# Rotary key rows by transfers on SyncE's queue, and four buffers for the squares of q blocks, in the opening of an attention stage

## The chip, the core and the metric

The kernel runs on one core of one Trainium2 chip. A core has TensorE (matmuls; PE in the profile, PEld its weight loads), VectorE (DVE), ScalarE (ACT), GpSimd (POOL) and SyncE (SP), which here only issues transfers. Each engine works through a list of instructions of its own in order; semaphores tie the lists together. Work tiles live in SBUF (128 partitions), results of matmuls in PSUM. The metric is the device time of one execution in microseconds (us), lower is better.

## The reference

One inference step of a two-layer decoder for a prompt of 1024 tokens (with 16 learned tokens ahead) and for 8 samples of 4 new tokens each. Layer A is a convolution module and a feed-forward network with a short convolution. Then one latent (128 wide) and one rotary key (32 wide) are formed for every token. Layer B attends to them and ends with a second feed-forward network. The part at hand, cut to what matters:

```python
q = einsum('btl,lhd->bthd', rms_norm(xn @ w_dq, ...), w_uq)      # 16 heads of 64 + 32
q_nope, q_rope = rms_norm(q[..., :64]), rope(rms_norm(q[..., 64:]))
k_nope = rms_norm(einsum('btc,chd->bthd', c, w_uk))              # from the latent c
v      = einsum('btc,chd->bthd', c, w_uv)
s = (q_nope . k_nope + q_rope . kr) * SM_SCALE                   # kr: one rotary key for all heads
o = softmax(causal(s)) @ v                                       # prompt
# samples: the same attention, over 2048 past tokens in 16 pages per sample and the 4 new ones
```

All in float32.

## The kernel before, in words

`run` calls, one after the other, the convolution phase, the first feed-forward network, `latents`, `attention` (the prompt), `samples`, `project` and the second feed-forward network. Precise products are made of three fast ones: `split` writes a tile as a high part (ACT, L135) and a low part (DVE, L136), and `mm3` multiplies high by high, low by high and high by low (L151).

**Order.** The text of the program is not the order on an engine. A planner with a timeline of its own sets each engine's list from priorities and from what has to be free: a tile can be written only when the last reader of whatever lay at its address before is done. `samples` opens under a high priority (`SPRIO`), so the planner lets its first instructions run among the last heads of `attention` wherever their tiles are free.

**Opening of attention.** `latents` leaves the rotary key rows of all 1040 tokens as a high and a low tile, kth0 and ktl0 (rows 0 to 31), and brings a copy to rows 32 to 63 of a second pair, kth1 and ktl1 (L1094). Attention keeps two sets of key tiles, so that one pair of heads can be prepared while another is in use; the second set (k2h, k2l, named `tiles`) needs the same rotary rows, copied at L1429 and L1431. In before GpSimd does all six copies. Heads go in groups of four. For a group, `group_k` makes keys (raw keys L1157, squares L1159, sums of squares L1160, norm L255 to L260, scaling L1169), `group_q` makes q in nine blocks of tokens: a block's matmuls (L151), two evictions by ACT (L1193, L1194), its squares by ACT (L1196), and their sums by DVE (L1200, L1201); then the norm and the rotation (`rope`, L1103 to L1107) on DVE. `query(n)` transposes the q of head n (L1277, L1280), `scores(n)` finds the largest score of each row (matmul L1307, maximum on DVE L1309 to L1314), `shift(n)` puts it into a row of q (L1323), and `values(n, g)` makes the weights (L1347 to L1350, exponential on ACT L1354) and the products with v (L1337). Opening means: all of group 0, then the nine blocks of group 1 woven into `query(0)` and `scores(0)`. From there the heads follow each other.

**Closing.** After heads 2p and 2p+1 their output is evicted into a tile `o` (L1364). Pairs 0 to 6 go through `finish` (division by way of GpSimd, then L1385 writes `o` to memory); pair 7, the last, through `close(7, 0)` and `close(7, 1)`: reciprocal (L1369) and product (L1370) on DVE, then a transfer on ACT's queue (L1371).

**Samples.** `samples` loads the key weights in two halves into tiles `rx` (L1516, on GpSimd's queue), splits them, turns the samples' q with them (24 small matmuls, `sn<-rx,wh` and the like), and goes through four pairs of samples: `scores(sp)` on pages that SyncE loads (`pg`, L613; splits `ch`, `cl`, and `kh`), `values(sp)` (L1629, L1640, L1651).

**Memory.** A pool is a stretch of SBUF with so many buffers of each tile's name, and pools are laid one behind the other in the order in which they are opened. In `attention` that is, at its end: `bp` (2 buffers; `scr` is there, a 1024-wide work tile that the squares of k and q and the rotation share), `bx` (`PB` = 4 buffers; weights `pf`), `ax` (`trit`, `pick`), `ao` (2 buffers of `o`). The pools of `samples` follow in the same memory.

Of the kernel before, what the change touches and what calls it, by code (L numbers as in the profile page):

```python
# [9 lines left out]
F32 = mybir.dt.float32  # L10
# [108 lines left out]
class Prog:  # L119
# [828 lines left out]
    def latents(self, es, eq, xh, xl, sq):  # L948
        nc, a, o = self.nc, self.a, self.o
# [8 lines left out]
        r = lambda w, n: aq.tile([128, w], F32R, name=n)  # L958
# [9 lines left out]
        with ExitStack() as e2:  # L968
# [113 lines left out]
            h, l = [t[64:96] for t in self.kt[0]]  # L1082
# [8 lines left out]
                for at, w, src in parts:  # L1091
                    self.split(h[:, at:at + w], l[:, at:at + w], ps[:32, src:src + w])
            for t, x in zip(self.kt[1], (h, l)):
                nc.gpsimd.tensor_copy(t[32:64], x.bitcast(F32))  # L1094

    def rope(self, tmp, kind, m, bs, n, d1, d2, x):
        nc = self.nc
# [11 lines left out]
    def attention(self, es):  # L1109
        nc, a = self.nc, self.a  # L1110
# [3 lines left out]
        bp = self.pool(es, "bp", 2)  # L1114
        bx = self.pool(es, "bx", PB)
# [7 lines left out]
        f32 = lambda shape, n, pool=at, **k: pool.tile(shape, F32, name=n, **k)  # L1123
# [9 lines left out]
        def sub(t, m, b0, nb, lo, step, w):  # L1133
            v = t[:m, b0:b0 + nb]
            return bass.AP(v.tensor, v.offset + lo, [list(v.ap[0]), [224, 2 * nb], [step, 2], [1, w]])

        def part(name, src, w, pool=ag):
            raw = f32([128, w], name + "r", pool)
            nc.sync.dma_start(raw, src)
            h, l = f32r([128, w], name + "h", pool), f32r([128, w], name + "l", pool)  # L1140
            self.split(h, l, raw)
            return h, l
# [36 lines left out]
        def group_q(g):  # L1179
            q = st["qn"] = f32([128, NB, 2, 224], f"q{g % 2}", au if g % 2 else ag)  # L1180
            ss, rr = f32([128, 2, 36], "ssq", al), f32([128, 2, 36], "rrq", al)
            nc.gpsimd.memset(ss, 1.0)
            nc.gpsimd.memset(q[:, :, :, 96:128], 0.0)
            wq = [part(f"wq{k}", a["wuq"][k][:, 384 * g:384 * g + 384], 384) for k in range(2)]
            yield
            for b in range(NB):
                m = 128 if b < 8 else 64
                c0 = 128 * b
                ps = (ps_p if g or b > EARLY else ps_f).tile([128, 512], F32, name="p")[:m, :384]
                for k in range(2):  # L1190
                    self.mm3(ps, self.qlh[k][:, c0:c0 + m], self.qll[k][:, c0:c0 + m], wq[k][0], wq[k][1], start=k == 0, stop=k == 1)
                v = ps.rearrange("p (r c) -> p r c", c=192)
                nc.scalar.activation(q[:m, b, :, 0:96], v[:, :, 0:96], AF.Copy)  # L1193
                nc.scalar.activation(q[:m, b, :, 128:224], v[:, :, 96:192], AF.Copy)  # L1194
                sc = f32([128, 1024], "scr", bp)[:, :384]
                nc.scalar.activation(sc[:m], ps, AF.Square)  # L1196
                sc = sc.rearrange("p (r c) -> p r c", r=2)
                w = ss[:m, :, 4 * b:4 * b + 4].rearrange("p k (r a) -> p k r a", a=2)
                for j, (lo, hi) in enumerate(((0, 64), (128, 192))):
                    nc.vector.tensor_reduce(out=w[:, 0, :, j], in_=sc[:m, :, lo:hi], op=ALU.add, axis=AX.X)  # L1200
                nc.vector.tensor_reduce(out=w[:, 1], in_=sc[:m, :, 64:128].rearrange("p r (a c) -> p r a c", a=2), op=ALU.add, axis=AX.X)  # L1201
                yield
            self.rsqrt(al, rr, [((ALL, i), ss[:, i], 1.0 / n) for i, n in enumerate((64, 32))], [128, 2, 36], "qa")
            yield

            def chunk(v, r, m, b0, nb, c, eng):
                s = lambda i, w: r(i).broadcast_to([m, c * nb // 2, 2, w])
                w = v(0, 160, 64)
                x = eng.tensor_tensor(out=w, in0=w, in1=s(0, 64), op=ALU.mult)
                for early in st.get("half", ()):  # L1210
                    self.after(x, early)
                yield
                w = v(64, 64, 32)
                t = f32([128, 1024], "scr", bp)[:m, :32 * c * nb].rearrange("p (a b) -> p a b", b=32)
                nc.vector.tensor_tensor(out=t.rearrange("p (a c) b -> p a c b", c=2), in0=w, in1=s(1, 32), op=ALU.mult)
                yield
                st["rope"] = self.rope(f32([128, 1024], "scr", bp), "q", m, slice(b0, b0 + nb), c, w[:, :, :, 0:16], w[:, :, :, 16:32],
                                       t.rearrange("p (a c) b -> p a c b", c=c))
                yield

            for r in () if g else range(2):
                for m, b0, nb in ((64, 8, 1), (128, 0, 8)):
                    def v(lo, step, w):
                        x = q[:m, b0:b0 + nb, r]
                        return bass.AP(x.tensor, x.offset + lo, [list(x.ap[0]), [448, nb], [step, 2], [1, w]])
                    s = lambda i: rr[:m, i, 4 * b0:4 * b0 + 4 * nb].rearrange("p (a c b) -> p a c b", c=4, b=1)[:, :, 2 * r:2 * r + 2]
                    yield from chunk(v, s, m, b0, nb, 2, nc.gpsimd if r else nc.vector)
                st["half"] = () if r else [st["rope"]]
                yield "half"
            for m, b0, nb in PIECES if g else ():  # L1230
                s = lambda i: rr[:m, i, 4 * b0:4 * b0 + 4 * nb].rearrange("p (a c b) -> p a c b", c=2, b=1)
                yield from chunk(lambda lo, step, w: sub(q, m, b0, nb, lo, step, w), s, m, b0, nb, 4, nc.gpsimd)
# [179 lines left out]
        def both(g):  # L1412
            yield from group_k(g)
            yield from group_q(g)

        gk, gq = group_k(0), group_q(0)
        for x, n in ((gk, 4), (gq, 4), (gk, 3), (gq, 6), (gk, 1)):
            for _ in range(n):
# [7 lines left out]
        for j, (h, l) in enumerate(self.kt):  # L1426
            r = (slice(64, 104), slice(0, 64))[j]
            h2, l2 = tiles[2 * j:2 * j + 2]
            nc.gpsimd.tensor_copy(h2[r], h[r].bitcast(F32))  # L1429
            r = (slice(64, 96), slice(0, 64))[j]  # L1430
            nc.gpsimd.tensor_copy(l2[r], l[r].bitcast(F32))  # L1431
            kts[0].append((h2, l2))
        nc.scalar.activation(pick, idn[0:8, 0:8], AF.Copy, scale=-1.0)
        nc.gpsimd.memset(mask[:, :KW - 128], 0.0)
# [7 lines left out]
        while next(gq) != "half":  # L1442
            pass
        nxt = group_q(1)
        for _ in range(1 + FILLQ):
            next(nxt)
# [445 lines left out]
```

## Time and profile before

| | us |
|---|---|
| median of 3 runs | 2760.52 (2760.06 to 2764.99) |
| the profiled execution | 2764.3 |
| its span in the trace | 2762.4 |
| granted TensorE clock, mean | 0.981 of full speed |
| PE busy in the span | 2652.8 |
| DVE busy | 1878.0 |
| ACT busy | 1356.2 |
| POOL busy | 711.0 |

In the trace, attention opens at about 1350 us, head 0's weights begin at 1419, the last product of attention starts at 1830 and the last one of the samples' pairs at 1919. A row of the timeline has start, duration, engine, line, operation, output and inputs by name (buffer numbers left out), shapes, a count where equal rows follow each other, and in brackets the idle time just before it with what ended it. Durations on PE run from start to modelled end, and consecutive matmuls overlap: the distance between starts is the time that one takes.

### The profile page before, as it was taken

How to read it: one execution, taken by the hardware profiler on the slowest of the kernel's cores; microseconds unless marked ns; L12 is line 12 of the kernel's file. 1: busy time of each engine (PE TensorE's matmuls, PEld its weight loads, DVE VectorE, ACT ScalarE, POOL GpSimd, SP SyncE). 2: the span in 40 equal slices, each digit the busy share in tenths (PEclk: the TensorE clock that was granted, in tenths of full speed). 3: DMA queues.
4: the chain of work that ended last, by engine and by line, in shares of the span. 5: the costliest groups of instructions: out<-in, count | busy, mean ns of one | idle time of the engine just before them, and what ended most of it. 6: DMA issues, size and time to landing. Idle time of an engine off the chain costs nothing.

```text
span 2762.4 us, 46569 instructions
## 1 busy us (share of the span) xinstructions
PE 2652.8 (96%) x16966; PEld 2448.0 (89%) x16966; DVE 1878.0 (68%) x3485; ACT 1356.2 (49%) x3701; POOL 711.0 (26%) x1019
## 2 busy tenths in 40 slices
PE   7999997999999999999889999999999999999999
PEld 6888876999999999999767776667999999999999
DVE  8899986578888875135677767676377777775232
ACT  6777775345444553023555555566245454453010
POOL 1567663024333330001111212110023333330000
PEclk9999997999999999999989999999999999999999
DMA  4211101502322236123100001267402222227122
GB/s 142 57 41 55 39 29 42 173 32 87 95 88 94 80 105 238 47 81 107 35 11 18 26 24 32 80 199 261 152 24 89 80 77 85 80 97 244 41 87 76
DMA packets 127769, 238.24 MB, mean 86 GB/s; under 512 B 39778, under 2 KB 81140, under 8 KB 127412
## 3 DMA queue, kind: packets, MB, share of 16 engines
q1 hardware_dynamic: 103828, 200.82, 22.6%
q0 software_dynamic: 9600, 32.36, 3.1%
q10 hardware_dynamic: 14112, 2.09, 0.5%
q8 instruction: 133, 2.18, 0.3%
q14 instruction: 96, 0.79, 0.1%
HBM read 183.90 MB, written 51.31 MB: 85 GB/s over the span
## 4 chain that ended last, share of the span: by engine, by line
PE 85%; DVE 6%; ACT 5%; DMA 2%; issue 2%; POOL 0%; SPq 0%; ACTq 0%; DVEq 0%; POOLq 0%
PE ps L796 30%; PE ps L175 22%; PE pk L654 5%; PE v L1337 5%; PE g L419 4%; PE ps L845 3%; PE p L151 2%; PE ps L197 2%; PE ps L1013 1%; PE po L1651 1%; PE p L1347 1%; PE p L1350 1%; PE p L1349 1%; PE s L1307 1%; PE sn L151 1%
## 5 line engine op out<-in xcount | busy, mean ns | idle before, releaser
L135 ACT ACTIVATE wh<-raw 128x512 fp32r<-128x512 f32 (+2 forms) x256 | 191.1, 749 | 542.0 <-PE ps L175 338.5
L136 DVE TENSOR_TENSOR wl<-raw,wh 128x512 fp32r<-128x512 f32 (+2 forms) x244 | 201.5, 829 | 111.4 <-ACT wh L135 109.2
L942 DVE TENSOR_TENSOR x<-ps,x 128x1074 f32<-128x1074 f32 (+1 forms) x48 | 61.0, 1270 | 293.1 <-PE ps L175 293.1
L766 DVE SCALAR_TENSOR_TENSOR c<-ub,c,c 128x1040 f32<-128x1040 f32 (+1 forms) x176 | 225.1, 1312 | 28.6 <-ACT c L763 27.6
L761 POOL COPY sb<-ub 128x32 f32<-128x32 f32 x88 | 88.8, 1011 | 400.9 <-DVE ub L807 363.2
L669 ACT ACTIVATE qq<-pk 128x64 f32<-128x64 f32 x736 | 158.1, 243 | 67.6 <-PE pk L654 67.5
L1337 PE MATMUL v<-pf,vf 128*128 128x512 f32 (+4 forms) x448 | 176.6, 478 | 10.0 <-ACT pf L1354 9.7
L663 POOL TENSOR_TENSOR sq<-sq 128x256 f32<-128x256 f32 (+4 forms) x229 | 140.2, 623 | 102.6 <-ACT sq L658 95.6
L175 PE MATMUL ps<-xh,wh 128*128 128x358 f32 (+1 forms) x672 | 148.3, 329 | 9.1 <-ACT xh L135 5.9
L1354 ACT ACTIVATE pf<-p 128x512 f32<-128x512 f32 (+4 forms) x224 | 99.0, 451 | 118.1 <-DVE p L1352 98.1
L669 ACT ACTIVATION_READ_ACCUMULATOR qq<-pk 128x1 f32 x736 | 153.9, 227 | 0.0
L523 DVE SCALAR_TENSOR_TENSOR a<-u,c,a 128x512 f32<-128x512 f32 x216 | 150.1, 745 | 4.9 <-ACT a L516 4.9
L175 PE MATMUL ps<-xh,wl 128*128 128x358 f32 (+1 forms) x672 | 147.6, 328 | 0.0
L175 PE MATMUL ps<-xl,wh 128*128 128x358 f32 (+1 forms) x672 | 147.4, 327 | 0.1
L175 PE MATMUL ps<-al,wh 128*128 128x358 f32 (+1 forms) x672 | 147.2, 327 | 0.0
L175 PE MATMUL ps<-ah,wl 128*128 128x358 f32 (+1 forms) x672 | 146.5, 326 | 0.0
L175 PE MATMUL ps<-ah,wh 128*128 128x358 f32 (+1 forms) x672 | 146.2, 326 | 0.0
L654 PE MATMUL pk<-ukh,ch 128*128 128x512 f32 x256 | 115.5, 452 | 25.6 <-ACT ch L135 13.4
L763 ACT ACTIVATE c<-ub,c 128x1074 f32<-128x1074 f32 (+1 forms) x88 | 101.3, 1185 | 59.7 <-DVE ub L807 46.8
L175 PEld LDWEIGHTS ps<-xh,wh 128*128 128x128 f32 x672 | 117.5, 191 | 12.7 <-ACT xh L135 6.8
L658 ACT ACTIVATE sq<-pk 128x512 f32<-128x512 f32 x164 | 99.8, 613 | 50.8 <-PE pk L654 48.5
L135 ACT ACTIVATE wh<-s 128x512 fp32r<-128x512 f32 x120 | 75.7, 631 | 94.9 <-PE ps L796 88.3
(599 smaller groups left out, 9100.4 us busy)
## 6 DMA issues: line engine op xcount, KB each, us to landing
raw<-wup SPq DMA_DIRECT2D x88, 512.0 KB, 3.5
pg<-ctn SPq DMA_DIRECT2D x128, 192.0 KB, 3.8
raw<-wdn SPq DMA_DIRECT2D x32, 448.0 KB, 3.3
raw<-pw SPq DMA_DIRECT2D x24, 512.0 KB, 3.9
d_a<-c POOLq DMA_DIRECT2D x22, 537.0 KB, 3.5
raw<-d_a SPq DMA_DIRECT2D x22, 537.0 KB, 5.2
d_a<-c POOLq DMA_DIRECT2D x22, 531.0 KB, 3.1
raw<-d_a SPq DMA_DIRECT2D x22, 531.0 KB, 5.3
```

The lines of the kernel that those rows point to most:

```text
L135: return (nc.scalar.activation(h, src, AF.Copy), (eng or nc.vector).tensor_tensor(out=l, in0=src, in1=h.bitcast(F32), op=ALU.subtract))
L136: (eng or nc.vector).tensor_tensor(out=l, in0=src, in1=h.bitcast(F32), op=ALU.subtract))
L175: nc.tensor.matmul(p[:, c, :ch], s[:, k * 128:(k + 1) * 128], m[k][:, off + c * ch:off + (c + 1) * ch], start=k == 0 and i == 0, stop=k == ...
L419: y = nc.tensor.matmul(p[:, 0], x[:, k * 128:(k + 1) * 128], m[k][:, t * ch:t * ch + ch], start=k == 0 and i == 0, stop=k == KD - 1 and i ...
L523: nc.vector.scalar_tensor_tensor(out=p[:, :ND] if j == n - 1 else acc, in0=x[:, j:j + ND], scalar=w[:, j:j + 1], in1=to if j == 1 else acc ...
L654: x = nc.tensor.matmul(ps, s[:, j, :], m[:, 512 * c:512 * c + 512], start=i == 0, stop=i == 2)
L663: nc.gpsimd.tensor_tensor(out=to, in0=v[:, :, :n], in1=v[:, :, n:2 * n], op=ALU.add)
L669: nc.scalar.activation(q, ps[:, 64 * h:64 * h + 64], AF.Square, accum_out=ss[:, p, 8 * c + h:8 * c + h + 1])
L763: x = nc.scalar.activation(c, ub, AF.Copy, scale=wd[:, t, 2:3])
L766: nc.vector.scalar_tensor_tensor(out=c[:, 2:pe], in0=ub[:, tap:tap + pe - 2], scalar=wd[:, t, tap:tap + 1], in1=c[:, 2:pe], op0=ALU.mult, ...
L796: nc.tensor.matmul(ps, w[:, s], m[:, lo:hi], start=first and k == 0 and i == 0, stop=k == KD // 2 - 1 and i == 2, skip_group_check=True)
L1337: nc.tensor.matmul(o[:, at_:], vf[:m, b, c], p[:m, :512 - at_], start=b == 0, stop=last)
```

## The change

Three places:

- L1094 (end of `latents`) and L1429, L1431 (opening of `attention`): the six copies of rotary rows are no longer GpSimd instructions but transfers from SBUF to SBUF on SyncE's queue.
- L1195: the squares of a q block are written to a tile of their own, `sqq` (384 wide), in the pool `bx`, which has four buffers, and no longer to `scr` in `bp`, which has two.

```diff
@@ latents
             for t, x in zip(self.kt[1], (h, l)):
-                nc.gpsimd.tensor_copy(t[32:64], x.bitcast(F32))
+                nc.sync.dma_start(t[32:64].bitcast(F32), x.bitcast(F32))
@@ group_q
-                sc = f32([128, 1024], "scr", bp)[:, :384]
+                sc = f32([128, 384], "sqq", bx)
                 nc.scalar.activation(sc[:m], ps, AF.Square)
@@ opening of attention
             r = (slice(64, 104), slice(0, 64))[j]
             h2, l2 = tiles[2 * j:2 * j + 2]
-            nc.gpsimd.tensor_copy(h2[r], h[r].bitcast(F32))
+            nc.sync.dma_start(h2[r].bitcast(F32), h[r].bitcast(F32))
             r = (slice(64, 96), slice(0, 64))[j]
-            nc.gpsimd.tensor_copy(l2[r], l[r].bitcast(F32))
+            nc.sync.dma_start(l2[r].bitcast(F32), l[r].bitcast(F32))
```

Where things lie after it: a buffer of `sqq` has 1536 bytes in each partition, four of them 6144, so all that is opened behind `bx` moves up by 6144 bytes. The second buffer of `o`, which pairs 1, 3, 5 and 7 use, lay at bytes 165792 to 169888 of each partition and now lies at 171936 to 176032. The tiles of `samples` stay where they were: `tm` at 171584 to 173632, `kn`, `knl`, `rxn` and `rtn` from 173632 to 174528, the first buffer of `rx` at 174528 to 176576. Before, none of these lay under `o`; now all of them lie under its second buffer, at least in part.

What this does to the engines' lists shows at three places. SyncE, opening of attention; kth and ktl are the rotary rows, 16158 and 16159 the first pair, 16160 and 16161 the second, the weights wq are those of group 1:

```order
 L1139 DMA uvr<-wuv 128x256
 L1139 DMA ukr<-wuk 128x256
+L1094 DMA kth_16160<-kth_16158 32x1040
+L1429 DMA k2h_17070<-kth_16158 40x1040
+L1094 DMA ktl_16161<-ktl_16159 32x1040
+L1431 DMA k2l_17071<-ktl_16159 32x1040
+L1429 DMA k2h_17072<-kth_16160 64x1040
+L1431 DMA k2l_17073<-ktl_16161 64x1040
 L1139 DMA wq0r<-wuq 128x384
 L1139 DMA wq1r<-wuq 128x384
```

The six transfers stand ahead of the loads of group 1's q weights.

GpSimd, last heads of attention; `rx<-wukt` is the load of the samples' key weights, `d_o<-o` the output of a pair. Before:

```order
611 L1209 TENSOR_TENSOR q_20030<-q_20030,rrq 64x2x2x64
612 L1381 DMA d_l<-lq 128x16
613 L1383 DMA lb<-d_l 64x1024 x2
614 L1384 TENSOR_TENSOR o<-o,lb 128x1024
615 L1516 DMA rx<-wukt 128x512 x2
616 L1524 MEMSET rs 128x512
617 L1576 DMA rk<-d_ss 128x512
618 L1385 DMA d_o<-o 128x1024
```

And with the change:

```order
624 L1384 TENSOR_TENSOR o<-o,lb 128x1024
625 L1385 DMA d_o<-o 128x1024
626 L1516 DMA rx<-wukt 128x512 x2
627 L1524 MEMSET rs 128x512
628 L1524 MEMSET rx 128x512
629 L1598 COPY rx<-rk 128x4x64 x32
```

The load stood behind pair 4's product; it now stands behind the last pair that GpSimd closes, pair 6.

PE, head 15, the last; `v<-pf,vf` is a product with v, `sn<-rx,wh` the first work of the samples. Before:

```order
7906 L1337 MATMUL v<-pf,vf 128x512
7907 L1347 MATMUL p<-qh,kth_16158 128x144
7908 L1349 MATMUL p<-qh,ktl_16159 128x144
7909 L1350 MATMUL p<-ql,kth_16158 128x144
7910 L151 MATMUL sn<-rx,wh 128x64
7911 L151 MATMUL sn<-rs,wh 128x64
7912 L151 MATMUL sn<-rx,wl 128x64
```

And with the change:

```order
7970 L1347 MATMUL p<-qh,kth_16160 16x16
7971 L1349 MATMUL p<-qh,ktl_16161 16x16
7972 L1350 MATMUL p<-ql,kth_16160 16x16
7973 L1337 MATMUL v<-pf,vf 128x272
7974 L1337 MATMUL v<-pf,vf 128x144
7975 L1337 MATMUL v<-pf,vf 128x16
7976 L151 MATMUL sn<-rx,wh 128x64
7977 L1559 MATMUL sn<-c_58,rxn 128x64
```

All matmuls of the samples that were woven among heads 14 and 15 now stand behind attention's last product.

## The prediction

> **What bounds the kernel now.** I read the page's head first, then the busy time of the engines in three stretches of the trace (opening of attention, last two heads, the four pairs of samples), then the timelines there. Columns of the windows: stretch, its length, busy time with count of PE, PEld, DVE, ACT, POOL, then granted clock, DMA share and GB/s.
>
> ```profile
> span 2762.4 us, 46569 instructions
> PE 2652.8 (96%) x16966; PEld 2448.0 (89%) x16966; DVE 1878.0 (68%) x3485; ACT 1356.2 (49%) x3701; POOL 711.0 (26%) x1019
> ...
> 1350.00:1419.00 69.00, 49.11 (x235) 39.37 (x233) 60.49 (x224) 39.83 (x112) 13.85 (x20) 0.83 0.14 39
> 1796.00:1831.00 35.00, 33.53 (x183) 24.85 (x181) 23.22 (x55) 22.80 (x52) 8.03 (x12) 1.00 0.38 114
> 1831.00:1920.00 89.00, 83.71 (x519) 64.96 (x518) 61.75 (x122) 63.92 (x150) 10.84 (x20) 0.96 0.87 287
> ```
>
> PE bounds the kernel as a whole, and it does so in the last two heads: 33.5 of 35 us. The opening is different: PE is busy for 49.1 of 69 us and DVE for 60.5. There DVE is nearly the bound, and any microsecond taken out of the opening reaches the end, since the heads behind it run on PE without slack. In the samples' stage the transfers are the busiest (0.87).
>
> **The opening: what it gains.** Rows of ACT, PE, DVE and POOL there:
>
> ```profile
> 1393.18 0.49 ACT L1196 ACTIVATE scr<-p 128x384 f32<-128x384 f32 x1 [4.40 <-DVE scr L1103]
> 1393.72 0.69 PE L151 MATMUL p<-wq0h,qlh 128*128 128x384 f32 x1 [5.53 <-ACT scr L1196]
> 1368.00 0.69 DVE L1160 TENSOR_REDUCE ssk<-scr 128x8 f32<-128x512 f32 x1 [1.10 <-ACT scr L1159]
> 1383.11 0.68 DVE L136 TENSOR_TENSOR k2l<-s,k2h 64x512 fp32r<-64x512 f32 x1 [1.91 <-ACT k2h L135]
> 1397.02 0.48 DVE L1200 TENSOR_REDUCE ssq<-scr 128x2 f32<-128x128 f32 x2 [1.29 <-ACT scr L1196]
> 1400.53 0.48 DVE L1200 TENSOR_REDUCE ssq<-scr 128x2 f32<-128x128 f32 x2 [1.11 <-ACT scr L1196]
> ...
> 1368.71 1.05 POOL L1094 CAST kth<-kth 32x1040 fp32r<-32x1040 f32 x1 [7.46 <-ACT kth L135]
> 1373.39 1.04 POOL L1429 CAST k2h<-kth 64x1040 fp32r<-64x1040 f32 x1
> 1371.07 1.03 DVE L255 TENSOR_SCALAR nr_v<-ssk 128x36 f32<-128x36 f32 x1
> 1372.14 1.06 DVE L256 TENSOR_SCALAR nr_y<-nr_v 128x36 int32<-128x36 int32 x1
> 1374.60 0.18 DVE L259 SCALAR_TENSOR_TENSOR nr_t<-nr_t,nr_v 128x36 f32<-128x36 f32 x1
> ```
>
> ACT waits 4.40 us for the rotation to leave `scr`, and PE waits 5.53 us for that square. With `sqq` this wait is gone. But the wait on PE is not the price: behind it stands DVE, whose work up to `shift(0)` (L1323, after which head 0 can begin) stays the same. What DVE gains is of two kinds. First its idle time, 8.5 of the 69 us: the four waits above make 5.4 of it. The three for ACT's squares (3.5 us) can go, the one for `k2h` stays. Second, while POOL's copies run (1368.7 to 1374.4), small DVE operations take 1.03 and 1.06 us, where their like takes 0.18 right behind. Four are hit; I count 0.85 for each of three and 0.6 for a larger one, 3.1 us.
>
> The Trainium skill (SBUF — State Buffer, Who interferes with whom) says that a DVE operation in a two-port mode or with two SBUF inputs and a GpSimd operation shut each other out for whole instructions; the trace agrees here, each hit operation having the length of one copy (1.03 beside 1.05). It names transfers as free of this, so by it too the 3.1 us go.
>
> The upper end of the gain is all idle time but the wait for `k2h`, 8.5 - 1.9, and the 3.1: about 10 us; the lower end is 2, if the stretched operations were not on the path. Against the upper end: in the changed list DVE has the sums of group 1's squares ahead of the rotation of head pair 0 and that rotation's second half ahead of `scores(0)`, so `query(0)` is not early by all of it. I take **5 us**, between the ends.
>
> The transfers themselves I cost at nothing:
>
> ```profile
> 1371.17 0.36 SPq L1139 DMA_DIRECT2D ukr<-wuk  x1
> 1377.90 0.33 SPq L1139 DMA_DIRECT2D wq0r<-wuq  x1
> 1400.40 0.58 PE L1307 MATMUL s<-k2h,qh 96*128 96x144 f32 x3
> ukr<-wuk SPq DMA_DIRECT2D x3, 128.0 KB, 2.3
> ```
>
> They stand behind the load of `ukr`, issued at 1371.2. Four issues of 0.36 follow, then the last two wait for the first and the third to land (2.3 us, by the nearest load): SyncE is through at about 1375.4, and all has landed by 1378. The rows are first read by `scores(0)`, at 1400. The loads of group 1's weights queue behind, but SyncE issued those only at 1377.9. Without that cover the cost is about 5 us for the chain of two.
>
> The Trainium skill (DMA: Bandwidth & Descriptors) gives a transfer a fixed cost of about 2.0 us, against 1.05 for a copy on POOL in this trace. By that rule alone the chain would be some 2 us longer than the copies; the slack until 1400 takes it.
>
> **The end of attention: what it costs.** The tile that the samples' weights are loaded into now lies under the `o` of the last pair, and the lists show it: PE's first samples' matmul stands behind attention's last product. Rows of before:
>
> ```profile
> 1796.79 0.24 PE L151 MATMUL sn<-rx,wh 128*128 128x64 f32 x1
> 1799.32 0.28 PE L151 MATMUL sn<-rx,wl 128*128 128x64 f32 x1
> 1805.01 0.50 PE L151 MATMUL sn<-ch,qth 128*128 128x512 f32 x1 [0.58 <-ACT pf L1354]
> 1829.91 1.27 PE L1337 MATMUL v<-pf,vf 128*128 128x272 f32 x6
> 1831.61 0.60 PE L1640 MATMUL pp<-c,s 128*128 128x128 f32 x4
> ...
> 1832.09 0.59 ACT L1364 ACTIVATE o<-v 64x512 f32<-64x512 f32 x1
> 1833.31 3.35 DVE L1369 RECIPROCAL l<-l 128x512 f32<-128x512 f32 x1 [2.79 <-ACT l L1364]
> 1823.07 0.69 DVE L1370 TENSOR_TENSOR o<-o,l 128x512 f32<-128x512 f32 x1
> d_o<-o ACTq DMA_DIRECT2D x2, 256.0 KB, 3.3
> rx<-wukt POOLq DMA_DIRECT2D x2, 256.0 KB, 3.5
> 1799.52 0.63 ACT L135 ACTIVATE wh<-tm 32x512 fp32r<-32x512 f32 x1 [1.83 <-PE sn L151]
> 1821.64 0.68 DVE L136 TENSOR_TENSOR cl<-pg,ch 128x512 fp32r<-128x512 f32 x1
> ```
>
> Call the end of attention's last product T; before it is 1831.2. With the change:
>
> 1. Where T goes. The samples' matmuls leave the stretch before it. By starts they take 2.8 us (24 from 1796.79 to 1799.5) and, at 0.23 to 0.25 a matmul, some 10.7 for the pages' blocks: 13.5. They also filled gaps of the heads; I give back 2.5. T = 1831.2 - 13.5 + 2.5 = 1820.2, less the 5 us of the opening.
> 2. From T to the samples' first page product. Eviction of `o` and `l` 1.2; reciprocal 3.35; product 0.7; its transfer 3.3; that is 8.5. Two issues and the landing of `rx` 1.2 + 3.5: 13.2. Splits of the second half 1.3, filling and splitting the samples' q 1.3: 15.7. The 24 matmuls 2.8: 18.5. Then as before from 1799.6 to 1805.0, 5.4: **24 us**, of which PE works for three.
> 3. `scores(0)` alone. DVE has 24 operations of 0.69 in its new list up to the first exponential, with the small ones 17.2; 4.1 of them belong to pair 1, which is work done ahead. So the state that before had at 1831.6 (first L1640) comes at T + 24 + 17.2 - 4.1 + 1 = T + 38.
> 4. The pairs. Their first L1640 before:
>
> ```profile
> 1863.95 0.60 PE L1640 MATMUL pp<-c,s 128*128 128x128 f32 x4
> 1886.31 0.60 PE L1640 MATMUL pp<-c,s 128*128 128x128 f32 x4
> 1907.40 1.97 PE L1640 MATMUL pp<-c,s 128*128 128x128 f32 x8 [1.01 <-ACT s L1629]
> 1918.88 0.65 PE L1651 MATMUL po<-cn,pt__23381 64*64 64x128 f32 x4
> ...
> 1829.84 10.10 SPq L613 DMA_DIRECT2D pg<-ctn  x16
> 1854.28 0.63 ACT L135 ACTIVATE ch<-pg 128x512 fp32r<-128x512 f32 x1 [2.50 <-DMA pg<-ctn]
> ```
>
> Pair 0 took 32.3 us, pairs 1 and 2 22.4 and 21.1, the rest 12. Pair 0 was long because 27 of pair 1's pages were issued only at 1829.84, when the last head's matmuls had freed their places (as the row of ACT shows, which waits 2.50 for one). With the change these places are free at about T, and the pages load during the 24 us of step 2. So pair 0 takes about 21.5, as the others: the stage gets back 11.
>
> The sum: 1820.2 + 38 - 1831.6 = 26.6 late at the first pair, 11 back, so **15 to 16 us** later at the samples' end, before the opening's 5. Net **+10 us**. On the profiled execution that is a span of 2772 for 2762.4 and a time of 2774 for 2764.3; on the median of the runs, which is 3.8 below the profiled one, **2770.5 us**.
>
> Bounds of the stall: if DVE alone set the pairs' pace (24 x 0.69 and small ones, and the exponential: 20.5 each) the stage gets back some 14, and 12 remain; if the pages that load during the closing slow the output's transfer and the weights', each to 5 us, and pair 0 keeps some of its waits, 24. Against the opening's 2 to 10 the net is +2 to +22.
>
> **Rivals.**
>
> *The pages' supply was the true bound of the samples* (faster). The DMA share of 0.87 from 1831 to 1920 speaks for it. All pages then go out earlier by the 11 us and the opening's share that T is earlier, pairs run at DVE's 17.2 us for one, and three pairs save 3 x 4.3 beyond my sum: 10.5 - 13 gives -3, and with the opening's full 10 it is **2752**. Against it: pairs 2 and 3 reuse the places of pairs 0 and 1, which are read until their `values` are done, and pairs 1 and 2 took 21 to 22 with few such waits.
>
> *The opening pays for the stall* (no change). With a gain of 10 and a loss of 11: **2761**. For it: PE is idle for 20 of 69 us in the opening. Against: DVE's order above, with 60.5 busy of 69.
>
> *The closing is slower than its parts* (slower still). Reciprocal, product, output, load and split are seven waits in a row on five engines; in before it went like this:
>
> ```profile
> 1837.96 0.69 DVE L1370 TENSOR_TENSOR o<-o,l 128x512 f32<-128x512 f32 x1
> 1840.36 0.33 ACTq L1371 DMA_DIRECT2D d_o<-o  x1
> ```
>
> The transfer was issued 9.2 us after T, where my sum has 5.2, since other work stood between. With these 4 us, and 5 for crowded transfers: 2770.5 + 9, **2780**.
>
> *The transfers don't do what they say*: SyncE's queue holds up group 1's weights. They would have to land 8 us later than I hold; then the opening's gain is lost, and the result is **2775**, within the range of my case.
>
> The rule on two-port operations gives no result of its own here.
>
> **How the numbers follow.** My case 0.55 (own range 2763 to 2778), the slower closing, with the held queue, 0.17, no change 0.14, the supply of pages 0.14. The range leaves out about 2 in 10: 2754 to 2782. About 0.2% (5.5 us) is what a measurement of this kernel can tell from no change. Of my case about 0.03 falls within it: faster 0.14, same 0.17, slower 0.69.
>
> **What would show it.** In the changed trace: no POOL copies at 1368, and no DVE operations stretched to 1.0 there; the 5.5 us wait of PE for a square gone; `shift(0)` about 5 us earlier. At the end: a PE gap of about 15 us between the last product of attention and `sn<-rx,wh`, ended by splits of the weights, `rx<-wukt` issued some 8 us after the last product, and pairs of about 21 us without waits for pages in pair 0. The prediction is wrong if that gap is under 8 us, if `shift(0)` is more than 10 us earlier, or if pair 0 still takes 30.

## The result and the profile after

The changed kernel takes 2788.24 us (median of 4 runs, 2787.4 to 2791.02) where the kernel before takes 2760.29 beside it: ratio 1.0098, 95% interval 1.0083 to 1.0113, slower by 27 to 28 us. The forecast was 2770.5 with a range to 2782: the sign held, the size did not. The profiled execution took 2791.02, its span is 2789.3 (before 2762.4).

The stretches of before, cut where they now begin and end (opening, last heads, the pairs of samples), and one that is new, from attention's last product to the first L1640; columns as in the prediction:

```profile
span 2789.3 us, 46580 instructions
...
1350.00:1414.00 64.00, 45.68 (x228) 34.72 (x226) 60.23 (x222) 37.69 (x108) 10.21 (x16) 0.87 0.22 59
1775.00:1810.00 35.00, 33.34 (x157) 22.19 (x155) 19.77 (x53) 18.21 (x43) 5.17 (x6) 1.00 0.73 224
1810.00:1863.00 53.00, 25.68 (x100) 19.91 (x101) 27.06 (x49) 25.00 (x52) 9.73 (x18) 0.65 0.37 123
1863.00:1945.00 82.00, 75.47 (x498) 61.95 (x496) 52.21 (x112) 55.15 (x131) 8.57 (x18) 0.96 0.71 237
```

The opening is shorter. A stretch of 53 us is new, in which no engine is busy for more than about half of the time and PE's granted clock is 0.65. The rows that bound it, from the timelines of PE, ACT, DVE and POOL:

```profile
1808.64 1.27 PE L1337 MATMUL v<-pf,vf 128*128 128x272 f32 x6
1809.94 0.59 ACT L1364 ACTIVATE o<-v 64x512 f32<-64x512 f32 x1 [0.67 <-PE v L1337]
1811.18 3.35 DVE L1369 RECIPROCAL l<-l 128x512 f32<-128x512 f32 x1 [2.03 <-ACT l L1364]
1815.34 0.33 ACTq L1371 DMA_DIRECT2D d_o<-o  x1
1819.85 0.84 ACT L1544 ACTIVATE tm<-qs 32x256 f32<-32x256 f32 x2 [8.69 <-DMA d_o<-o]
1820.39 1.11 POOL L1516 DMA_DIRECT2D rx<-wukt  x2 [24.71 <-DVE rxn L1556]
1826.43 0.63 ACT L135 ACTIVATE wh<-rx 128x512 fp32r<-128x512 f32 x1 [1.21 <-DMA rx<-wukt]
1827.94 0.39 PE L151 MATMUL sn<-rx,wh 128*128 128x64 f32 x1 [18.04 <-ACT rx L135]
1838.94 0.79 PE L151 MATMUL sn<-ch,qth 128*128 128x512 f32 x1 [4.20 <-ACT qth L135]
1862.66 0.60 PE L1640 MATMUL pp<-c,s 128*128 128x128 f32 x4
```

Read from top to bottom this is the chain of step 2 of the prediction: last product, eviction, reciprocal, output (whose landing frees ACT and the load), weights, splits, and only then PE's next matmul, after 18.04 us of idling. ACT's wait of 8.69 us for `d_o<-o` shows what holds the samples: the output tile of the last pair lies where their tiles have to be written.

The opening, by the rows that answer to those of before:

```profile
1367.87 0.17 DVE L255 TENSOR_SCALAR nr_v<-ssk 128x36 f32<-128x36 f32 x1
1368.07 0.18 DVE L256 TENSOR_SCALAR nr_y<-nr_v 128x36 int32<-128x36 int32 x1
1402.21 1.62 PE L1307 MATMUL s<-k2h,qh 96*128 96x272 f32 x3 [6.29 <-DVE ql L138]
L1323 DVE TENSOR_TENSOR qh<-p,pick x16: 1202/1215/1218, 1412.8 to 1790.6; 8x1024 fp32r<-8x1024 f32 x16
```

The operations that took 1.03 and 1.06 us beside POOL's copies take 0.17 and 0.18. PE's wait of 5.53 us for a square is gone, and one of 6.29 us for DVE stands in `scores(0)` instead. Head 0's shift (first of the 16 in the last row) is at 1412.8, before at 1417.7: 4.9 us earlier. Of these, 0.6 come from ahead of the opening: the last matmul of `latents` (L1013) starts at 1350.8 before and at 1350.2 here. From there to the shift it is 66.9 us before and 62.6 here, 4.3 less. (Below, the three other runs with this opening, experiments 8 to 10, have 62.6 as well, and the two with the opening of before, 3 and 4, have 68.0 and 66.4.)

Part of what PE waits for there is a new stretching. One small operation of the rotation, 0.18 us long before, now takes 4.54, from the start to the end of four products on POOL (two of L1169, two of L1209). In before the same four products ran beside sums of squares on DVE, which kept their usual 0.48. The changed kernel first, then before:

```profile
1391.83 4.54 DVE L1103 TENSOR_TENSOR scr<-scr,tabqcos 64x32 f32<-64x32 f32 x1
1391.83 2.27 POOL L1169 TENSOR_TENSOR k<-k,rrk 64x128 f32<-64x128 f32 x2 [16.36 <-DVE scr L1215]
1394.06 2.26 POOL L1209 TENSOR_TENSOR q<-q,rrq 64x128 f32<-64x128 f32 x2
...
1393.91 2.27 POOL L1169 TENSOR_TENSOR k<-k,rrk 64x128 f32<-64x128 f32 x2 [11.50 <-DVE q L1107]
1394.38 0.48 DVE L1200 TENSOR_REDUCE ssq<-scr 128x2 f32<-128x128 f32 x2
```

### The profile page after: what moved, and what is told of

The parts are those of the page before. It is cut to its first block, busy times and chain, and to the rows that moved or that the text cites. A ratio compares the mean times of both kernels' runs of the same rounds, so it can differ in the third digit from the quotient of the medians.

```text
span 2789.3 us, 46580 instructions
## 1 busy us (share of the span) xinstructions
PE 2648.9 (95%) x16966; PEld 2442.9 (88%) x16966; DVE 1881.7 (67%) x3485; ACT 1356.8 (49%) x3701; POOL 704.9 (25%) x1013
## 4 chain that ended last, share of the span: by engine, by line
PE 83%; DVE 7%; ACT 5%; DMA 3%; issue 2%; SPq 0%; POOL 0%; ACTq 0%; DVEq 0%; POOLq 0%
PE ps L796 30%; PE ps L175 22%; PE pk L654 5%; PE v L1337 4%; PE g L419 4%; PE ps L845 3%; PE p L151 2%; PE ps L197 2%; PE ps L1013 1%; PE p L1347 1%; PE p L1350 1%; PE p L1349 1%; PE s L1307 1%; PE po L1651 1%; PE sn L151 1%
```

## The experiments

The theory after the result, called **memory** below: the whole loss comes from the address of the output tile, not from the transfers or the squares. The rivals: the transfers cost it by SyncE's queue; the squares' own tile costs it; or the planner, given another layout, sets a worse order in general.

**1. The transfers alone.** The squares stay in `scr`:

```diff
-                sc = f32([128, 384], "sqq", bx)
+                sc = f32([128, 1024], "scr", bp)[:, :384]
```

> The six transfers alone; the squares stay in the shared work tile, so the output tile of the last pair stays where it was. Memory theory (the whole loss comes from the address of that tile): no gap of PE behind attention's last product, first L1640 at about 1829, VectorE's stretched operations gone, 2757 to 2760 (the 3.1 us of stretching at most). Transfer theory (SyncE's queue costs the time): 2775 or more, with the first samples' product late.

Measured 2756.11 (9 runs) beside 2761.27 for before: ratio 0.998, interval 0.9968 to 0.9992. So the transfers make the kernel faster, by about 5 us (2 to 9). The samples' first matmul is back among the last heads, and the first L1640 follows on attention's last product:

```profile
1787.19 0.24 PE L151 MATMUL sn<-rx,wh 128*128 128x64 f32 x1
1822.31 1.27 PE L1337 MATMUL v<-pf,vf 128*128 128x272 f32 x6
1824.01 0.60 PE L1640 MATMUL pp<-c,s 128*128 128x128 f32 x4
1367.18 0.17 DVE L255 TENSOR_SCALAR nr_v<-ssk 128x36 f32<-128x36 f32 x1
1367.38 0.18 DVE L256 TENSOR_SCALAR nr_y<-nr_v 128x36 int32<-128x36 int32 x1
```

The transfer theory falls.

**2. The squares alone**, GpSimd copying as before: the diff of the change at L1195 and nothing else.

> The squares' own tiles alone, in the pool with the weights; the six copies stay on GpSimd. Memory theory: the 18 us gap behind attention's last product is there, first L1640 at 1862 to 1866; about 2791, that is the changed kernel without what the transfers give (2 to 3 us). Transfer theory: near 2760.

Measured 2793.01 (4 runs) beside 2761.27, ratio 1.0117 (1.01 to 1.0133), with the first L1640 at 1862.0 as expected. The loss goes with this edit.

**3. The shift alone**: the kernel before, with an empty tile of 6144 bytes.

```diff
         bx = self.pool(es, "bx", PB)
+        self.pool(es, "gap2", 1).tile([128, 1536], F32, name="gap2")
         ax = self.pool(es, "ax", 1)
```

> The kernel before with nothing but 6144 bytes left empty in each partition behind the pool of the weights. No instruction is added or removed. Memory theory: the opening is as before (shift of head 0 at 1417.7), and the whole loss is there without the opening's gain of 4.9 us: about 2793. Rival (the new tiles or the transfers themselves delay something): 2760, since nothing is computed or moved differently.

Measured 2792.43 (4 runs) beside 2761.27, ratio 1.0106 (1.009 to 1.0121). No operation is added or removed, nothing is computed elsewhere, and it loses what the change loses. (Head 0's shift was at 1414.9 and not at 1417.7, since this execution came to the opening 3.9 us earlier; the opening itself was no shorter, 68.0 us from L1013 on.) PE's gap is the same:

```profile
1812.28 1.27 PE L1338 MATMUL v<-pf,vf 128*128 128x272 f32 x6
1832.34 0.39 PE L151 MATMUL sn<-rx,wh 128*128 128x64 f32 x1 [18.78 <-ACT rx L135]
```

By the medians, each beside its own before, the shift costs 31 us and the change 28. The difference of 3 fits what the transfers give by themselves, but the intervals (1.009 to 1.0121 and 1.0083 to 1.0113) overlap, so the times alone do not show it. Experiments 2 and 3 differ by 0.6 us with runs that spread over 6 to 8, so whether the squares alone give something cannot be seen here.

**4. Half the shift**: the same with 768 in place of 1536 columns. The last pair's output then covers part of `tm`, not the tiles of the key weights.

> The kernel before with 3072 empty bytes behind the pool of the weights, half of the change's shift and nothing else. The output tile of the last pair then ends at byte 172960: it covers part of tm, but not the tiles that the samples' key weights are loaded into. Memory theory: the load of those weights and the 24 small matmuls stay among the last heads as before, only what hangs on tm (the rotary part of the samples' q) waits for the last pair's output, some 10 us after attention's last product: a loss between, 2770 to 2785. Rival (any shift of this size moves the planner to a worse order, whatever lies where): a loss of the same 31 us, 2792; or the loss grows in step with the bytes, 2776 by chance of the same size but with the key weights late.

Measured 2779.4 (4 runs) beside 2761.18, ratio 1.0066 (1.0048 to 1.0084): 18 us. The key weights are early, `tm` waits:

```profile
1790.59 0.24 PE L151 MATMUL sn<-rx,wh 128*128 128x64 f32 x1
1823.97 0.84 ACT L1545 ACTIVATE tm<-qs 32x256 f32<-32x256 f32 x2 [8.63 <-DMA d_o<-o]
```

So what counts is which tile is covered, not that something moved. That the loss went from 31 to 18 when the bytes were halved would fit a loss in step with the bytes as well; the rows speak against that, and so does the next experiment.

**5. A quarter of the shift, with both edits**: one buffer for the squares, 1536 bytes, in a pool of its own at the same place. Then no tile of the samples is covered. (The "variant behind the output tiles" that the expectation names is experiment 6.)

```diff
+        bs = self.pool(es, "bs", 1)
         ax = self.pool(es, "ax", 1)
-                sc = f32([128, 384], "sqq", bx)
+                sc = f32([128, 384], "sqq", bs)
```

> Both edits, with a single buffer for the squares, 1536 bytes in place of 6144: the output tile of the last pair ends at 171424 and covers none of the samples' tiles. Memory theory: no gap at the end, the opening as in the transfers alone or up to 2 us better, 2753 to 2757. Rival (a squares tile of its own costs time in the opening, as in the variant behind the output tiles): 2763.

Measured 2759.23 (12 runs) beside 2761.18, ratio 0.9993 (0.9981 to 1.0005). The loss is gone altogether, as memory has it, and not reduced to a quarter: attention's last product starts at 1828.1 and the first product with the weights (L1641 in this kernel) at 1829.8. But the gain is not clear either: the time lies above what was expected, and some 3 us above the transfers alone by the medians.

**6. The squares behind the output tiles**, four buffers, so that `o` keeps its address:

```diff
         ao = self.pool(es, "ao", 2)
+        bs = self.pool(es, "bs", PB)
-                sc = f32([128, 384], "sqq", bx)
+                sc = f32([128, 384], "sqq", bs)
```

> Both edits, but the four buffers of the squares in a pool of their own opened behind the output tiles, which so keep their address. Memory theory: the opening as in the changed kernel (shift of head 0 at 1412.8), the samples' opening as before: 2755.5, 4.9 us faster than before. Rival (squares or transfers cost time by themselves): over 2765.

Measured 2763.46 (11 runs) beside 2761.27, ratio 1.0006 (0.9996 to 1.0016): no loss, and no gain, so the expectation of 2755.5 was missed. The end is right (the first L1640 follows at once on attention's last product). The opening is not. ACT's first square, PE's last transposes of the rotary rows:

```profile
1364.07 0.61 PE L1088 MATMUL ps<-c,ko 128*32 128x128 f32 x4 [0.49 <-DVE ktl L136]
1365.87 0.45 PE L151 MATMUL p<-wq0h,qlh 128*128 128x384 f32 x1 [1.19 <-ACT sqq L1197]
1368.83 0.48 DVE L1201 TENSOR_REDUCE ssq<-sqq 128x2 f32<-128x128 f32 x2 [1.52 <-ACT sqq L1197]
```

Under one of the four buffers, the one of the second square, lay `ko`, the rotated keys of `latents`, which L1088 reads until 1364.7. The first two squares began together at 1365.3, right behind that; in the changed kernel the first began 7 us earlier, at 1358.6. The first square's buffer holds nothing of `ko`; the planner's list puts it behind the same readings, and why is not shown. The opening, 62.6 us from L1013 to head 0's shift in the changed kernel, takes 66.0 here. The tiles had been taken out of the way of the stage behind and put into that of the stage ahead.

**7. The squares in the output tiles**, which nothing else uses until head 0 is done; not a byte more is needed.

```diff
-                sc = f32([128, 384], "sqq", bx)
+                sc = (f32([128, SEQ], "o", ao) if g < 2 else f32([128, 1024], "scr", bp))[:, :384]
```

> Both edits of the opening without a byte more: the squares of groups 0 and 1 go to the two output tiles, which nothing else uses before head 0 is done; later groups use the shared work tile as before. Memory theory: no stall at the end, and the transfers' gain of 5 us plus whatever the squares give in the opening (0 to 3 us): 2752 to 2756. Rival (squares apart from the shared tile give nothing or cost, as one buffer did): 2756 to 2760.

Measured 2758.68 (12 runs) beside 2761.64, ratio 0.9991 (0.9978 to 1.0004). Three ways to part the squares from `scr` without the stall now stand at -2, +2 and -3 us beside before, the transfers without them at -5. The squares' own tile gives nothing that can be measured, and may cost a little.

The traces show where its gain went. From L1013 to head 0's shift, in before, with the transfers alone, with both edits and with the squares alone (columns as before: PE, PEld, DVE, ACT, POOL):

```profile
1350.80:1417.70 66.90, 47.71 (x228) 38.25 (x227) 58.53 (x219) 39.26 (x112) 13.71 (x20) 0.83 0.14 40
1347.50:1410.80 63.30, 46.39 (x228) 37.27 (x227) 55.43 (x219) 39.11 (x112) 7.41 (x14) 0.85 0.22 60
1350.20:1412.80 62.60, 44.91 (x227) 34.27 (x225) 58.89 (x221) 37.31 (x107) 8.84 (x15) 0.88 0.22 60
1345.60:1411.10 65.50, 47.90 (x228) 37.84 (x226) 61.97 (x221) 38.16 (x108) 15.25 (x20) 0.84 0.15 41
```

The transfers take 3.1 us off DVE's work and leave its idle time at 7.9 of 8.4 us. The squares' tile takes 4.2 us of idle time away and adds 3.5 of work, so that 0.7 are left. The work added is the one rotation operation beside POOL's four products, 4.36 us over its usual 0.18; the rest of DVE's work up to the shift is 0.9 less. That operation takes 4.54 us in the changed kernel, 4.53 and 4.54 in experiments 5 and 6, 4.47 in experiment 2 and 3.06 here, where it begins 1.5 us behind the first product and ends with the last. In before and with the transfers alone, where the order on DVE has sums beside these products, it is not stretched. How much of the times of experiments 5 to 7 this explains is open, as their heads differ by some us too.

**8 and 9. Keeping PE warm.** In the gap the granted clock falls to half. The stretches of 1815 to 1821, 1828 to 1834 and 1834 to 1839 in the changed kernel:

```profile
1815.00:1821.00 6.00, 0.00 (x0) 0.00 (x0) 0.52 (x3) 1.11 (x4) 0.60 (x2) 0.50 0.94 310
1828.00:1834.00 6.00, 5.93 (x27) 5.68 (x28) 0.61 (x2) 0.56 (x2) 0.97 (x3) 0.50 0.44 157
1834.00:1839.00 5.00, 0.80 (x5) 0.40 (x3) 1.20 (x3) 4.83 (x10) 1.64 (x4) 0.50 0.00 0
```

The 24 small matmuls, 2.8 us before, take 5.7. The Trainium skill (TensorE: Matmul & The Clock Gate, What's actually happening) says that the array falls to half its clock after an idle window of about 3.4 us; the trace agrees: PE is idle from 1809.9, and the granted clock is 0.88 from 1810 to 1815 and 0.50 from 1815 on. To see what this costs, matmuls without use were added in the gap, 24 and then 12 (each shows as two in the profile's counts):

```diff
                 close(n // 2, 1)
+                pw = ps_p.tile([128, 512], F32, name="p")
+                for _ in range(24):
+                    nc.tensor.matmul(pw, idn, st["l", n // 2][:, 512:], start=True, stop=True)
```

> The changed kernel with 24 matmuls added that compute nothing that is used (identity times the last pair's sums, into a spare PSUM tile). They fill TensorE's gaps between attention's last product and the samples' first page products. Clock theory (after the idle gap TensorE is granted half speed, and the samples' opening pays 6 to 9 us for it): the 24 small matmuls take 2.8 us in place of 5.7, first L1640 some 5 us earlier, 2781 to 2784. Rival (the samples' opening is a chain through DVE and ACT, the clock costs nothing that shows): 2787 to 2790.

> The changed kernel with 12 added matmuls that compute nothing that is used, in the gap behind attention's last product; 24 of them had run 3 us into the samples' own work, 12 take about 12 us of the 13 that are free. Clock theory (half speed after the idle gap costs time at the end): the 24 small matmuls in 2.8 to 3.2 us, first page product 3 us and first L1640 3 to 6 us nearer to attention's last product, 2782 to 2786. Rival (the chain through ACT and DVE hides the slower matmuls): 2787 to 2790.

Measured 2787.97 beside 2761.18 (ratio 1.0094, 1.0075 to 1.0112) and 2790.66 beside 2761.64 (1.0089, 1.0065 to 1.0114), 4 runs each: no gain that can be seen. With 24 the added work ran until 1827.8, about 3 us past the time at which the samples' weights were ready, and its rest stood ahead of the first page product, from 1831.6 to 1837.2. With 12 it did what it should in the first gap:

```profile
1811.93 1.27 PE L1337 MATMUL v<-pf,vf 128*128 128x272 f32 x6
1817.88 12.75 PE L1490 MATMUL p<-l,c 128*128 128x512 f32 x24 [4.68 <-DVE l L1369]
1831.78 0.27 PE L151 MATMUL sn<-rx,wh 128*128 128x64 f32 x1 [1.15 <-ACT rx L135]
1835.01 0.28 PE L151 MATMUL sn<-rx,wl 128*128 128x64 f32 x1
1840.37 0.80 PE L151 MATMUL sn<-ch,qth 128*128 128x512 f32 x1 [4.59 <-ACT qth L135]
1864.17 0.60 PE L1643 MATMUL pp<-c,s 128*128 128x128 f32 x4
```

The small matmuls take 3.5 us, the first page product comes 27.2 us after the last product (1813.2) in place of 29.0, the first L1640 after 51.0 in place of 52.8. So the part of the slow clock that was taken away costs some 2 us at the first L1640, below the 3 to 6 that the clock theory wanted. The clock fell to 0.50 again behind the small matmuls (1840.3 to 1846.0 in this run), so what all of it costs is not shown; no difference in the whole time can be seen.

**10. Without the pages of pairs 2 and 3.** The changed kernel; these pairs read the pages of pairs 0 and 1 again.

```diff
         def fetch(sp, e, g):
             slot = NP * (2 * sp + e) + 4 * g
+            if sp > 1:
+                return st["pg", sp - 2, e, g]
```

> The changed kernel with the page loads of sample pairs 2 and 3 left out: these pairs read the pages of pairs 0 and 1 again, so their outputs are not the reference's. Supply theory (after the stall pairs 1 and 2 take 24 us in place of 21 to 22 because pages are still being loaded): both pairs at 20 to 22, 2783 or less. Rival (the order of work that the planner chose makes them 24): no change, 2788.

Measured 2785.32 (4 runs, 2784.27 to 2785.42) beside 2761.64: 2.9 below the changed kernel by the medians, and above the 2783 that the supply theory wanted; the ratios' intervals, 1.0056 to 1.0097 and 1.0083 to 1.0113, overlap. The pairs by their first L1640, of the changed kernel (first three rows, after 1862.66) and of this one:

```profile
1884.25 0.60 PE L1640 MATMUL pp<-c,s 128*128 128x128 f32 x4
1908.56 0.60 PE L1640 MATMUL pp<-c,s 128*128 128x128 f32 x4
1932.60 0.66 PE L1640 MATMUL pp<-c,s 128*128 128x128 f32 x4 [0.43 <-ACT s L1629]
```

```profile
1863.84 1.05 PE L1642 MATMUL pp<-c,s 128*128 128x128 f32 x4
1886.43 0.60 PE L1642 MATMUL pp<-c,s 128*128 128x128 f32 x4
1908.26 0.66 PE L1642 MATMUL pp<-c,s 128*128 128x128 f32 x4
1928.36 1.36 PE L1642 MATMUL pp<-c,s 128*128 128x128 f32 x8 [0.43 <-ACT s L1631]
```

Pairs 0, 1, 2: 21.6, 24.3, 24.0 with the loads, 22.6, 21.8, 20.1 without. Pairs 1 and 2 lose 6.4 us and the whole stage 5; ACT's waits for pages (up to 2.25 us, in pair 2) are gone. In this trace supply sets the pace of pairs 1 and 2 after the stall; the whole time does not show it clearly. Supply means both the transfers and the wait for a place to load into, since the edit takes away both.

## Why the prediction was half right

Sign and cause were right: the opening gains, the covered tile costs, and the covered tile costs more. The size was not. The stall was put at 15 to 16 us and bounded at 24; the shift alone costs 31 (experiment 3). The step that failed is the third, `scores(0)` alone, with smaller misses in steps 2 and 4. By the prediction's own steps (times of the two profiled executions):

| step | forecast | measured |
|---|---|---|
| opening, shift of head 0 | 5 earlier | 4.9 earlier (4.3 in the opening itself) |
| 1. last product T (opening included) | 1815.2 | 1809.9 |
| 2. T to the first page product | 24 | 29.0 |
| 3. on to the first L1640 | 14 (18.2 less 4.1 of credit) | 23.7 |
| 4. pair 0 | 21.5 | 21.6 |
| 4. pairs 1 and 2 | 22.4, 21.1 | 24.3, 24.0 |

- **The opening** was right in size, and in part by luck. DVE's work got shorter by 3.1 us with the transfers alone (experiment 7), which is the stretching that the prediction had counted, and PE's wait for the square did not become a gain, since DVE stood behind it. The six transfers are hidden: those whose landing the trace shows took 2.4 to 3.0 us, and `scores(0)` begins at 1395.6. But the idle time that the squares' tile took away from DVE was mostly paid back by one rotation operation stretched to 4.54 us beside POOL's products, a cost that stands nowhere in the prediction; that the result lies so near to 5 is owed to it. Of the 4.3 us, 3.6 come with the transfers alone. Had the prediction parted the edits, it would have seen that one carries the gain and the other the loss.
- **Step 1** took too little away: between head 0's shift and T lie 413.5 us before and 397.1 after, 16.4 less, where it had 11 (13.5 less 2.5 given back). T came 5.3 us sooner than forecast.
- **Step 2** had the right links and two that were too short. The output landed in 4.3 us in place of 3.3 and the weights in 4.8 in place of 3.5, while pages were loading at a DMA share of 0.94; that the loading slowed them was not tested. And the half clock doubled the 24 matmuls, 2.9 us, of which some 2 reach the first L1640 (experiment 9).
- **Step 3 failed.** It priced `scores(0)` at DVE's work alone, 18.2 us for that stretch, as if DVE were never idle. Alone, without heads to run beside, the stage is a ring of ACT, PE and DVE, each waiting for the one before: 23.7 us, in which DVE was busy for 18.9 and idle for 4.8. It also took 4.1 us of credit for work done ahead for pair 1. But step 4 priced pair 0 at 21.5 us by pairs that begin with such work done as well (in before, DVE has four of pair 2's operations behind it, 1858.5 to 1861.7, when pair 1's largest scores are ready at 1862.0), so the same work was counted twice. Together 9.7 us.
- **Step 4** was right on pair 0 and wrong behind it. After a shorter pair 0 the next pages come late: 2.0 and 2.9 us more than before in pairs 1 and 2, which experiment 10 ties to the loads.

The sum: 5.3 us better in step 1; 5.0, 9.7 and 4.8 worse in the others; that is 14 of the 17 us between the forecast's 10 and the span's 27. Of the rest, 1.7 lie behind pair 3's first product (856.7 us to the end of the span, 855.0 before), less than executions of one kernel differ by; the remainder is rounding in the forecast.

Of the signs that the prediction had named, most came: the gap (18 us for about 15), the load of the weights issued 10.5 us behind the last product for some 8, pair 0 at 21.6. Pairs 1 and 2, at 24, did not. None of its signs of being wrong came. They asked whether the stall is there, and none looked at `scores(0)`, where the largest part of the miss lies.

Of the rivals, the slower closing (2780) was nearest and named the crowded transfers, but not the main part of the miss. The prediction's reading of the samples' stage, that the transfers are the busiest there, does not follow from its row: PE is busy for 83.7 of the 89 us, 0.94, against 0.87. The supply of pages came true in the other direction: not as a bound that hides the stall, but as one that keeps it from being made good.

The fastest version that was run is the transfers alone, 2756.11, ratio 0.998 (0.9968 to 0.9992) to the kernel before.

## What to carry to other kernels

A new buffer moves every tile that is laid out behind it, and the price appears where the next stage wants to start early under the tail of this one: compare which tiles lie over which, at both ends of a stage, before pricing the edit itself. A stage that has run in another's shadow must not be priced by its busiest engine alone when it loses the shadow; here it then paid 4.8 us of waits between its engines on top of DVE's 18.9. And where one change has several edits, price and run them apart: here one gave 5 us and the other took 31.

## What was not expected

- 6144 bytes that nothing reads or writes cost 31 us of 2761 (experiment 3), and 3072 cost 18.
- The clock is at half, 0.50 from 1815 to about 1844 in the changed kernel, and the 24 small matmuls take twice as long; bringing them back to full clock brought the first L1640 only some 2 us nearer (experiment 9).
- Beside POOL's copies a small DVE operation of 0.18 us takes 1.03 to 1.06, and without them 0.17 to 0.18 (experiment 1): that is 3.1 of the 3.6 us by which the transfers alone shorten the opening.
- Beside four POOL products in a row, a DVE operation of 0.18 us took 4.54, as long as all four together. It stands there in every kernel that was run with the squares apart from `scr`, shorter in experiment 7 alone, and in the changed kernel it ate most of what the squares' tile had to give.
